# A hybrid decoder layer on one core: short matmul operands filled up with zero rows, and four stretches reordered

## The chip, the core and the metric

The kernel runs on one core of one Trainium2 chip. The metric is device microseconds of one execution of the whole program. The kernel before took 2721.23 us (median of 3 runs, 2720.73 to 2722.72). A core has five engines that run side by side, each with its own instruction queue: TensorE (PE; its weight loads are listed as PEld), VectorE (DVE), ScalarE (ACT), GpSimd (POOL) and SyncE (SP), which here only starts transfers.

## What is computed

One layer of a decoder trunk, for 1024 prompt tokens with 16 learned meta tokens ahead of them, and for a sample group of 8 sequences with 8 tokens each (1104 tokens in all, width 1024). Cut to its parts:

```
h = h + 0.5 * post1(swiglu1(pre1(h)))                  # d_ff 2816
u = pre_mix(h);  qkv, z, b, a, sq, sk, sv, g_dn, g_swa = split(u @ w_in)
A: gated DeltaNet, 8 heads of 128 (chunks for the prompt, a recurrence from a given
   state s0 for each of the 8 sample sequences), gated RMSNorm with silu(z)
B: sliding-window attention, window 128 plus the 16 meta keys, 8 query heads
y = sigmoid(g_dn) * o_A + sigmoid(g_swa) * o_B
h = h + post_mix(y @ w_out)
h = h + 0.5 * post2(swiglu2(pre2(h)))
```

Besides y the outputs are the convolution, DeltaNet and window states of both groups.

## The kernel before, in words

**Order of work.** TensorE's instructions run in the order in which the program is written; the other engines' order is chosen when the program is built, except where an instruction is pinned to program order. The written order comes from `weave`: each stream of work is a generator with a start share, an end share and a number of steps, and the steps of all streams are merged by these shares. A projection of 72 or 73 steps is typically the filler between the dependent steps of another stream. The products of activations by weights are done in three fast passes (high by high, high by low, low by high parts); the small products of the mixer are plain float32 and appear in the trace as two matmul records each.

**Stages, with the time from the span's start.** First FFN: gate and up to about 485 us, `Ffn.down` (L511) to about 765. The last feature group of `down` ends in 24 steps; then each of nine token tiles (eight of 128, one of 80 tokens) is turned to token rows by `end` (L588, transposes L579), normed and added (`post_norm`: ACT square L81, two POOL instructions, DVE L625 and L626), stored, normed again (`pre_norm`, DVE L100) and transposed back in two steps (PE L104, then ACT L119 and DVE L120). `tail_steps` takes a list: a number is `end` of that tile, a pair such as (0,) one step of its `pre_norm`, None nothing. The lists stand in `body` beside `weave`, and in the three lists handed to `Mixer.before` (L795), where the filler is the first projections.

**Keys.** `all_keys` (L1026) projects the eight heads' keys one after the other. The generator `gates` (L813) has four steps and computes decays from a small product: matmuls L820; a long run of small DVE instructions; matmuls L858 to L863 with DVE L866; then ACT L870, the transpose L872, a store and six ACT exponentials. The first runs beside the first weave, the other three beside the projection of key head 2.

**Window attention.** `swa_block` (L1194) runs 32 times, from about 1055 to 1315 us. Its last step (L1252) accumulates four to seven products in one bank; the first of them has 48 rows: the 16 meta keys' values `vm` in three parts, by the transposed probabilities `ptm`. `swa_sample` (L1258) runs twice, each time with two halves; a half has four pairs of matmuls (L1311 with 128 rows, L1312 with 24 rows), each pair on its own 32 columns of the array. The triangular solves of the DeltaNet (`lane_solve`, DVE L1061 and L1063) run beside the first half of this stage.

**Heads.** `heads` (L1634) runs eight heads from about 1337 to 1880 us. Per head: `chain` (L1515, 29 steps, each waiting for the one before through ACT and DVE), `prep` and `prep8` of the next head, `emit` of the head before, and two projections as filler (`qv_steps`, `z_gate`). The sample group's part has 64 token rows and 16 meta rows: L1502 makes p8, L1543 solves with 80 rows, L1549 starts the state S from the 16 meta rows, L1552 makes the outputs from 64 rows, L1600 updates the eight sequences' states twice per head, 4 sequences at a time, from 64 rows of kd by `xe` (POOL L1559: the solution repeated eight times under `smask`). `emit` transposes the outputs (L1617; the sample's from partitions 64 to 127).

**Merge.** `z_gate` of the last head also loads `w_out` piece by piece (`load_w` L1686) into the memory of activations that are no longer needed. `begin` and `begin_last` do tile 0, `run` the others in the order 4, 1, 5, 2, 8, 6, 3, 7: `load` (L1786) brings y of all eight heads with one transfer, ACT L1715 and DVE L1716 split it, `tile_` (L1798) multiplies the two halves of the output one after the other.

The lines that speak most of the order around the change:

```
dn = f1.down(GROUPS, [(accp, (1, 2, 5, 7, 3, 6, 4))], hbp)
weave((dn, 0, 1, 15), ends(0, None, 1, None, None, (0,), (0,), 2, None, (1,), (1,), 3))
m.before([[ends((2,), (2,), 4, (3,), (3,), 5)], [ends((4,), (4,), 6, (5,), (5,), 7, 8)],
          [ends((6,), (6,), (7,), (7,), (8,), (8,))]])
```

Of the kernel before, what the change touches and what calls it, by code (L numbers as in the profile page):

```python
# [13 lines left out]
ALU = mybir.AluOpType  # L14
# [60 lines left out]
def rstd(c, pool, x, n, scale, eps, tag, dump=None, pin=lambda op: op):  # L75
# [5 lines left out]
    c.last_square = pin(nc.scalar.activation(dump[:n], x[:n], AF.Square, accum_out=r[:n])).ins  # L81
    nc.gpsimd.tensor_scalar(out=r[:n], in0=r[:n], scalar1=scale, scalar2=eps, op0=ALU.mult, op1=ALU.add)
    c.last_factor = nc.gpsimd.tensor_tensor(out=r[:n], in0=r[:n], in1=c.mhalf[:n, 0:1], op=ALU.pow).ins
# [87 lines left out]
class Ffn:  # L171
# [325 lines left out]
    def down(self, groups, accp, hbp):  # L497
# [9 lines left out]
        for vi, group in enumerate(groups[:-1]):  # L507
# [10 lines left out]
            for p in runs:  # L518
# [22 lines left out]
             for name in ("11", "21", "12", "22")}  # L541
        adds = [[(pool, 6, 1), (dve, 2, 1)], [(dve, 3, 5), (pool, 7, 6)], [(dve, 3, 6)], [(pool, 4, 7)], [(dve, 5, 7)], [], [],
# [110 lines left out]
C_BASE = C_SMASK + 8  # L653
# [5 lines left out]
def constants():  # L659
# [14 lines left out]
    cst[:64, C_SMASK:C_SMASK + 8] = seq[:64, None] == np.arange(8)[None, :]  # L674
# [19 lines left out]
class Mixer:  # L694
    def __init__(self, c, xT, I, O, es, ba_w):
# [10 lines left out]
        self.smask = t([P, 8], "smask")  # L706
        nc.sync.dma_start(self.smask, I["cst"][:, C_SMASK:C_SMASK + 8])
# [91 lines left out]
    def before(self, rest):  # L799
# [6 lines left out]
        with tc.issue_after(self.c.last_square), tc.issue_after(self.c.last_factor):  # L806
            self.ready[9] = self.w_in(9, raw[1])
# [5 lines left out]
    def gates(self, tp):  # L813
# [31 lines left out]
        for m in (15, 13, 11, 9, 7, 5, 3):  # L845
# [8 lines left out]
                                in1=self.smask[:80].unsqueeze(2).to_broadcast([80, 8, H]), op=ALU.mult)  # L854
# [171 lines left out]
    def all_keys(self):  # L1026
        c = self.c
        with ExitStack() as ek:
# [3 lines left out]
            with ExitStack() as eg:  # L1032
# [5 lines left out]
                before = [(gates, 0.5, 1, 3)]  # L1038
# [61 lines left out]
    def swa_kv(self, pool, tmp):  # L1100
# [6 lines left out]
        self.vm = c.t(pool, [48, 256], F32R, tag="vm")  # L1107
# [53 lines left out]
        nc.vector.tensor_copy(self.vm, vm)  # L1161
# [30 lines left out]
    def swa_block(self, t, p, pool):  # L1192
# [37 lines left out]
        pm = c.t(pool, [48, 2, P], F32R, tag="ptm", bufs=2)  # L1230
        nc.scalar.copy(pm, pt[:48, 0:2])
# [34 lines left out]
    def swa_sample(self, g, pool, tmp):  # L1266
# [27 lines left out]
        for half in range(2):  # L1294
# [109 lines left out]
    def persistent(self, pool):  # L1404
        c, nc = self.c, self.nc
        self.ms = [c.t(pool, [P, 8, P], tag=f"ms{i}") for i in range(1)]
        self.p8 = [c.t(pool, [64, P], tag=f"p8{i}") for i in range(2)]
        for m in self.ms + self.p8:
            nc.gpsimd.memset(m, 0.0)
# [68 lines left out]
    def prep8(self, h, pool):  # L1478
# [8 lines left out]
        kd = x["kd8"] = T([P, P], "kd8")  # L1487
        nc.sync.dma_start(kd, self.kd_d[h][:, 8, :])
        s0 = x["s0"] = T([P, 8, P], "s0")
# [13 lines left out]
        nc.vector.scalar_tensor_tensor(out=p8[:, 64:P], in0=pk[:64, 0, 0:64], scalar=self.s[:64, h, 8:9], in1=dt8,  # L1503
# [3 lines left out]
        self.pack8(x8, x["cv"])  # L1507
        vs = x["vs8"] = T([P, P], "vs8")
# [5 lines left out]
    def chain(self, h, pool):  # L1514
# [4 lines left out]
        vs, kd, s0, ms, p8 = (x[k] for k in ("vs8", "kd8", "s0", "ms", "p8"))  # L1519
# [35 lines left out]
        on = T([P, 1, P], "on8")  # L1555
        normed(o, slice(64, P), 8, 0, on)
        x["on"].append((on, 8, 1, 64))
        xe = T([64, 8, P], "xe")
# [580 lines left out]
```

## Time and profile before

| | |
|---|---|
| median of 3 runs | 2721.23 us |
| the profiled execution, device time | 2728.27 us |
| its span in the trace | 2726.4 us |
| mean granted TensorE clock | 0.989 of full |
| PE, PEld busy | 2644.8 us (97%), 2483.8 us (91%) |
| DVE, POOL, ACT busy | 1554.8, 1309.5, 1112.8 us |

The profiled execution is 7.0 us longer than the median of the runs. In the trace a PE row's duration overlaps that of the next row, since matmuls are pipelined; what an instruction costs is read from the starts. A form such as 48\*128 48x256 means 48 rows and 128 stationary columns, 256 moving columns; x2 at the end of a row means two records.

### The profile page before, as it was taken

To read this page: it belongs to the slowest core of one execution; us is meant where nothing else is said; L and a number is where in the kernel's file an instruction comes from. 1 tells how busy PE (TensorE), PEld (TensorE's weight loads), DVE (VectorE), ACT (ScalarE), POOL (GpSimd) and SP (SyncE) were. 2 spreads that over 40 slices of the span, in tenths; PEclk is the share of its full clock that TensorE was granted. 3 is DMA by queue.
4 is the path that set the end of the run, shared out by engine and by line. 5 is a ranking of instruction groups with operands and counts; after the bars stand their busy time and mean duration, and the time that the engine had idled before them with its cause. 6 is when DMAs were issued, how large, how long until landed. Compare 5 with 4: busy or idle time off the path is not lost. (4 is left out here: it accounts for less than half of the span.)

```text
span 2726.4 us, 49217 instructions
## 1 busy us (share of the span) xinstructions
PE 2644.8 (97%) x18957; PEld 2483.8 (91%) x18957; DVE 1554.8 (57%) x2294; ACT 1112.8 (41%) x2647; POOL 1309.5 (48%) x1227
## 2 busy tenths in 40 slices
PE   7999999999989998999999999998999999999998
PEld 7999999999978997887788888886789999999998
DVE  7656566446566769934354444443556556563566
ACT  6334343422145634555444444444543333344221
POOL 6655555445426733423344443344456555554471
PEclk9999999999999999999999999999999999999999
DMA  4344343677544743443333333334443344338764
GB/s 168 105 155 158 121 157 114 254 232 243 176 132 144 237 137 112 144 150 111 87 90 97 98 95 93 97 96 136 136 137 140 121 153 159 131 122 310 240 235 141
DMA packets 229552, 406.46 MB, mean 149 GB/s; under 512 B 59734, under 2 KB 121334, under 8 KB 229030
## 3 DMA queue, kind: packets, MB, share of 16 engines
q1 hardware_dynamic: 209014, 324.75, 36.9%
q10 hardware_dynamic: 20304, 78.56, 7.3%
q8 instruction: 150, 2.46, 0.4%
q14 instruction: 84, 0.69, 0.1%
HBM read 264.36 MB, written 140.53 MB: 149 GB/s over the span
## 5 line engine op out<-in xcount | busy, mean ns | idle before, releaser
L132 PE MATMUL gu<-xh,wl 128*128 128x512 f32 (+3 forms) x1456 | 497.3, 342 | 0.2 <-POOL wl L764 0.2
L128 PE MATMUL gu<-xh,wh 128*128 128x512 f32 (+3 forms) x1456 | 493.8, 339 | 0.0
L130 PE MATMUL gu<-xl,wh 128*128 128x512 f32 (+3 forms) x1456 | 493.4, 339 | 0.0
L282 POOL TENSOR_TENSOR wl<-T,wh 128x512 fp32r<-128x512 f32 x246 | 330.9, 1351 | 323.8 <-ACT wh L281 242.5
L492 PE MATMUL y<-hb,wh 128*128 128x256 f32 (+2 forms) x2528 | 430.6, 290 | 6.9 <-DMA hb<-hid 4.7
L282 POOL TENSOR_TENSOR wl<-raw,wh 128x512 fp32r<-128x512 f32 x200 | 282.8, 1422 | 257.5 <-ACT wh L281 202.4
L492 PEld LDWEIGHTS y<-hb,wh 128*128 128x128 f32 x2528 | 365.8, 188 | 9.0 <-DMA hb<-hid 4.5
L132 PEld LDWEIGHTS gu<-xh,wl 128*128 128x128 f32 x1456 | 277.7, 191 | 28.9 <-issue 11.1
L281 ACT CAST wh<-T 128x512 fp32r<-128x512 f32 x246 | 152.4, 620 | 369.3 <-PE B L316 114.3
L130 PEld LDWEIGHTS gu<-xl,wh 128*128 128x128 f32 x1456 | 278.1, 191 | 18.9 <-issue 1.2
L128 PEld LDWEIGHTS gu<-xh,wh 128*128 128x128 f32 x1456 | 278.0, 191 | 18.4 <-issue 1.6
L492 PE MATMUL y<-hb,wl 128*128 128x256 f32 (+2 forms) x1264 | 271.5, 288 | 0.0
L281 ACT CAST wh<-raw 128x512 fp32r<-128x512 f32 x200 | 122.3, 620 | 276.3 <-PE C L316 86.7
L503 DVE TENSOR_TENSOR acc<-acc,y 128x552 f32<-128x552 f32 (+4 forms) x216 | 144.9, 679 | 145.2 <-PE y L492 144.8
L764 POOL TENSOR_TENSOR wl<-raw,wh 128x1024 fp32r<-128x1024 f32 x60 | 146.5, 2441 | 160.2 <-ACT wh L763 153.3
L492 PEld LDWEIGHTS y<-hb,wl 128*128 128x128 f32 x1264 | 207.0, 188 | 0.0
L256 DVE TENSOR_TENSOR T<-raw,raw 128x512 f32<-128x512 f32 x124 | 118.8, 962 | 114.7 <-POOL wl L282 114.7
L1530 POOL TENSOR_TENSOR f<-f,mhalf 128x1 f32<-128x1 f32 (+1 forms) x72 | 54.8, 761 | 112.6 <-DVE f L1528 107.3
L267 DVE TENSOR_TENSOR T<-raw,T 128x512 f32<-128x512 f32 x62 | 64.4, 1041 | 62.7 <-POOL wl L282 62.3
L922 DVE SCALAR_TENSOR_TENSOR cv<-pc,cw,cv 128x1131 f32<-128x1131 f32 x48 | 67.0, 1397 | 29.3 <-POOL cv L919 28.9
L256 DVE TENSOR_TENSOR T<-raw,T 128x512 f32<-128x512 f32 x62 | 64.3, 1044 | 33.6 <-POOL wl L282 33.4
L1061 DVE TENSOR_TENSOR ltmp<-la 72x14 f32<-72x14 f32 (+37 forms) x76 | 69.6, 916 | 12.7 <-DMA la<-b_d 11.3
(588 smaller groups left out, 7323.7 us busy)
## 6 DMA issues: line engine op xcount, KB each, us to landing
hb<-hid SPq DMA_DIRECT2D x71, 552.0 KB
hb<-hid SPq DMA_DIRECT2D x71, 544.0 KB
hid<-hs ACTq DMA_DIRECT2D x69, 552.0 KB
hid<-hs ACTq DMA_DIRECT2D x69, 544.0 KB
raw<-in_w_in_dram SPq DMA_DIRECT2D x58, 512.0 KB
raw<-in_ffn_w_gate_dram SPq DMA_DIRECT2D x100, 256.0 KB
raw<-in_ffn_w_up_dram SPq DMA_DIRECT2D x94, 256.0 KB
raw<-in_ffn_w_down_dram SPq DMA_DIRECT2D x88, 256.0 KB
```

The lines of the kernel that those rows point to most:

```text
L128: nc.tensor.matmul(ps, wh, xh, start=first and i == 0, stop=False)
L130: nc.tensor.matmul(ps, wh, xl, start=False, stop=False)
L132: nc.tensor.matmul(ps, wl, xh, start=False, stop=last and i == n - 1)
L256: pin(self.nc.vector.tensor_tensor(out=b[name], in0=b[x], in1=b[y], op=ALU.subtract))
L267: nc.vector.tensor_tensor(out=s, in0=b["21"], in1=s, op=ALU.subtract)
L281: self.nc.scalar.copy(hi, s)
L282: self.nc.gpsimd.tensor_tensor(out=lo, in0=s, in1=f32(hi), op=ALU.subtract)
L492: self.nc.tensor.matmul(self.view(ps[d], (i,)), w[x][:, d * P:(d + 1) * P], hb[:, y, lo:hi], start=j + x + y == 0, stop=j == len(items) - ...
L503: dve = lambda out, x, y: nc.vector.tensor_tensor(out=out, in0=x, in1=y, op=ALU.add)
L764: nc.gpsimd.tensor_tensor(out=lo, in0=raw, in1=f32(hi), op=ALU.subtract)
L922: nc.vector.scalar_tensor_tensor(out=cv, in0=pc[:, w:w + PADW], scalar=self.cw[:, j, w:w + 1], in1=cv, op0=ALU.mult, op1=ALU.add)
L1061: nc.vector.tensor_tensor(out=t, in0=a[:n, 0:j, j:j + 1].to_broadcast([n, j, w]), in1=a[:n, j:j + 1, j + 1:size].to_broadcast([n, j, w]), ...
```

## The change

It does six things. (1) Operands with 16, 24, 48 or 64 rows become operands of 80 or 128 rows whose added rows are zero, or lie where full-height operands are read: `vm` and `ptm` (now two buffers zeroed once), p8, the stationary side of L1502, the transposes of the sample outputs. The 24-row matmuls L1312 stay, but the four L1311 of a half are issued first and then the four L1312. (2) The mask that picked a sequence moves from the moving operand (`xe`, POOL, removed) to the keys: `kds`, nine masked copies of the 80 key rows made on ACT in `prep8`, pinned to program order; a product with 512 moving columns becomes four with 128. (3) In the first `down`, the hidden values of the last two products get four buffers of their own in the memory of the raw weights, one PSUM pool is given up two steps earlier, and the lists of tile steps change. (4) The second step of the four of `gates` is placed at 0.5 of the next projection, the last two at 0.99. (5) The last head's `z_gate` ends at 0.95 of the chain in place of 0.85. (6) The merge's tile 4 is loaded, split and multiplied in two parts: heads 0 to 6, then head 7, both output halves in each.

```diff
@@ Ffn.down
-    def down(self, groups, accp, hbp):
+    def down(self, groups, accp, hbp, last_hbp=lambda hbp: hbp):
...
+        hbp2 = last_hbp(hbp)
...
-        second = [self.values(hbp, group, p) for p in (8, 4)]
+        second = [self.values(hbp2, group, p) for p in (8, 4)]
...
-                for ds in ((0, 1), (2,), (3,)) if i == 0 and q == 4 else ((0,), (1,), (2,), (3,)):
+                for ds in ((0, 1), (2,), (3,)) if i == 0 and q == 4 and hbp2 is hbp else ((0,), (1,), (2,), (3,)):
@@ Mixer.before
-        with tc.issue_after(self.c.last_square), tc.issue_after(self.c.last_factor):
+        with tc.issue_after(self.c.squares[-2]), tc.issue_after(self.c.factors[-2]):
@@ all_keys
-                before = [(gates, 0.5, 1, 3)]
+                before = [(steps_of(gates, 1), 0.4, 0.6, 1), (gates, 0.98, 1, 1)]
@@ swa_kv, swa_block
-        self.vm = c.t(pool, [48, 256], F32R, tag="vm")
+        self.vm = c.t(pool, [P, 256], F32R, tag="vm")
+        self.pm = [c.t(pool, [P, 2, P], F32R, tag=f"ptm{i}") for i in range(2)]
+        for x in (self.vm, *self.pm):
+            nc.gpsimd.memset(f32(x), 0.0)
...
-        pm = c.t(pool, [48, 2, P], F32R, tag="ptm", bufs=2)
-        nc.scalar.copy(pm, pt[:48, 0:2])
+        pm = self.pm[t % 2]
+        nc.scalar.copy(pm[0:48], pt[:48, 0:2])
@@ swa_sample
                 nc.tensor.matmul(po[r], p[:, 0, r], vc[:, i, :], start=True, stop=False, tile_position=(0, 32 * i))
+            for i in range(4):
+                r = slice(32 * i, 32 * i + 32)
                 nc.tensor.matmul(po[r], p[:24, 1, r], v24[:, i, :], start=False, stop=True, tile_position=(0, 32 * i))
@@ prep8
+        kds = x["kds"] = T([80, 9, P], "kds")
+        def masked(ss):
+            for s in ss:
+                c.tc.keep_in_program_order(nc.scalar.activation(kds[:, s], kd[:80], AF.Copy,
+                                                                scale=self.smask[:80, s:s + 1]))
...
+        masked(range(4))
...
-        nc.tensor.matmul(pk[:64, 0, 0:64], kq[:, 0:64], kq[:, 64:P], start=True, stop=True)
+        nc.tensor.matmul(pk[:, 0, 0:64], kq, kq[:, 64:P], start=True, stop=True)
...
+        masked(range(4, 9))
@@ chain
-        nc.tensor.matmul(pu, kd[64:80], xs8[64:80], start=True, stop=True)
+        nc.tensor.matmul(pu, kds[:, 8], xs8[:80], start=True, stop=True)
...
-        nc.tensor.matmul(po, p8, xs8[0:64], start=True, stop=True)
+        nc.tensor.matmul(po, p8, xs8[:80], start=True, stop=True)
...
-        nc.gpsimd.tensor_tensor(out=xe, in0=xs8[0:64].unsqueeze(1).to_broadcast([64, 8, P]),
-                                in1=self.smask[:64].unsqueeze(2).to_broadcast([64, 8, P]), op=ALU.mult)
...
-                nc.tensor.matmul(pu, x["kd8"][0:64], xe[:, 4 * half:4 * half + 4, :], start=True, stop=True)
+                for s in range(4):
+                    nc.tensor.matmul(pu[:, s, :], kds[:, 4 * half + s], xs8[:80], start=True, stop=True)
@@ emit
-                r = slice(0, P) if w == P else slice(64, P)
-                nc.tensor.transpose(pt[:, i, :w], on[r, i, :], self.k(C_IDENT)[r, r])
+                nc.tensor.transpose(pt[:, i, :], on[:, i, :], self.k(C_IDENT))
@@ heads
-                streams += [(self.z_gate(H - 1, pool, mg.load_w), 0, 0.85, 145), (steps_of(out, 2), 0.6, 1.15, 2)]
+                streams += [(self.z_gate(H - 1, pool, mg.load_w), 0, 0.95, 145), (steps_of(out, 2), 0.6, 1.15, 2)]
@@ Merge.load, Merge.tile_
+        for ks in (slice(0, H - 1), slice(H - 1, H)) if t == 4 else (slice(0, H),):
+            nc.sync.dma_start(f32(yl)[:, ks, :n], y[ks, :, t % 4 * P:t % 4 * P + n].rearrange("h p t -> p h t"))
...
+        if t == 4:
+            both = [c.t(self.psum, [P, 512], tag="dn", bufs=2) for _ in range(2)]
+            for ks in (range(H - 1), range(H - 1, H)):
+                for half in range(2):
+                    yield from self.mm(both[half], yh, yl, half, n, ks, ks.start == 0, ks.stop == H)
+                    if ks.stop == H:
+                        self.nc.scalar.copy(o[:n, half * 512:(half + 1) * 512], both[half])
@@ body
-        drain(steps_of(dn, 10))
+        drain(steps_of(dn, 8))
...
-        weave((dn, 0, 1, 15), ends(0, None, 1, None, None, (0,), (0,), 2, None, (1,), (1,), 3))
+        weave((dn, 0, 1, 17), ends(0, 1, None, None, None, (0,), (0,), 2, (1,), (1,), 3, None, None, (2,), (2,), 4))
...
-        m.before([[ends((2,), (2,), 4, (3,), (3,), 5)], [ends((4,), (4,), 6, (5,), (5,), 7, 8)],
-                  [ends((6,), (6,), (7,), (7,), (8,), (8,))]])
+        m.before([[ends(5, (3,), (3,), 6, (4,), (4,))], [ends(7, (5,), (5,), 8, (6,), (6,))],
+                  [ends(None, (7,), (7,), None, (8,), (8,))]])
```

## Rows read from the trace of the kernel before

**Rows 1.** The page, part 1: busy time, share of the span, instructions.

```profile
PE 2644.8 (97%) x18957; PEld 2483.8 (91%) x18957; DVE 1554.8 (57%) x2294; ACT 1112.8 (41%) x2647; POOL 1309.5 (48%) x1227
```

**Rows 2.** PE's waits, 730 to 850 us: total us, times, longest.

```profile
PE tr L872 <- ACT gc L870: 4.5, 1, 4.5
...
PE y L492 <- DMA hb<-hid: 1.7, 2, 1.3
```

**Rows 3.** Stretches: length, busy PE, PEld, DVE, ACT, POOL (instructions), granted clock, DMA, GB/s.

```profile
765.00:815.00 50.00, 39.29 (x304) 36.96 (x304) 31.36 (x35) 25.30 (x50) 17.10 (x33) 0.93 0.46 148
...
835.00:850.00 15.00, 10.52 (x53) 9.79 (x53) 9.72 (x11) 5.87 (x17) 4.81 (x8) 0.77 0.41 111
1000.00:1140.00 140.00, 131.50 (x808) 117.60 (x807) 136.41 (x189) 55.86 (x160) 53.18 (x48) 0.98 0.34 106
...
1340.00:1860.00 520.00, 517.68 (x3412) 453.37 (x3412) 231.18 (x489) 232.12 (x758) 211.21 (x254) 1.00 0.32 93
1860.00:1880.00 20.00, 14.72 (x81) 12.42 (x82) 9.46 (x22) 9.64 (x28) 16.00 (x16) 0.83 0.32 100
1888.00:1896.00 8.00, 5.23 (x16) 3.61 (x15) 2.65 (x3) 4.22 (x6) 1.87 (x3) 0.79 0.92 314
```

**Rows 4.** Timeline of PE, a window block: start us, us, line, operands, records.

```profile
1092.48 0.39 PE L132 MATMUL gu<-xh,wl 128*128 128x512 f32 x1
1092.80 0.38 PE L1252 MATMUL po<-ptm,vm 48*128 48x256 f32 x1
...
1093.92 0.40 PE L128 MATMUL gu<-xh,wh 128*128 128x512 f32 x1
```

**Rows 5.** Timeline of PE, one half of the sample attention.

```profile
1207.81 0.41 PE L1311 MATMUL po<-kc,pts 128*32 128x128 f32 x2
...
1210.48 0.41 PE L128 MATMUL gu<-xh,wh 128*128 128x320 f32 x1
1210.73 0.31 PE L130 MATMUL gu<-xl,wh 128*128 128x320 f32 x1
```

**Rows 6.** Timeline of PE, the sample scores: four column tiles, issued together.

```profile
1182.10 0.47 PE L1287 MATMUL sc<-kc,qp 128*32 128x152 f32 x8
1182.49 0.50 PE L128 MATMUL gu<-xh,wh 128*128 128x512 f32 x1
```

**Rows 7.** Timeline of PE, a state update with 64 rows.

```profile
1358.77 0.40 PE L128 MATMUL gu<-xh,wh 128*128 128x512 f32 x1
1359.00 0.40 PE L130 MATMUL gu<-xl,wh 128*128 128x512 f32 x1
1359.33 1.12 PE L1600 MATMUL on<-xe,kd 64*128 64x512 f32 x2
...
1360.72 0.40 PE L128 MATMUL gu<-xh,wh 128*128 128x512 f32 x1
```

**Rows 8.** Timeline of PE, the products with 16 and 64 rows.

```profile
1343.15 0.39 PE L130 MATMUL gu<-xl,wh 128*128 128x512 f32 x1
1343.47 0.48 PE L1549 MATMUL ch<-xs,kd 16*128 16x128 f32 x2
...
1344.63 0.28 PE L128 MATMUL gu<-xh,wh 128*128 128x256 f32 x1
```

**Rows 9.** Timeline of PE, the solve with 80 rows.

```profile
1340.83 0.39 PE L130 MATMUL gu<-xl,wh 128*128 128x512 f32 x1
1341.06 0.38 PE L1543 MATMUL ch<-vs,r 80*80 80x128 f32 x2
...
1341.51 0.40 PE L128 MATMUL gu<-xh,wh 128*128 128x512 f32 x1
```

**Rows 10.** ACT's scaled copy of one line: duration ns min, median, max; first and last start.

```profile
L1531 ACT ACTIVATE on<-o,f x72: 389/402/427, 1347.0 to 1877.7; 128x128 f32<-128x128 f32 x64, 64x128 f32<-64x128 f32 x8
```

**Rows 11.** PE's waits, 1858 to 1900 us: total us, times, longest.

```profile
PE ch L1584 <- ACT xs L1581: 3.4, 4, 2.0
```

**Rows 12.** Timeline of ACT, 1858 to 1900 us: start us, us, line, operands, instructions.

```profile
1868.80 1.65 ACT L1698 CAST xh<-raw 128x512 fp32r<-128x512 f32 x3
```

More of the change, by code (lines that the diff above doesn't have):

```diff
@@ L80, in rstd @@
         dump = c.t(pool, [P, D], BF16, tag="dump", bufs=1)
-    c.last_square = pin(nc.scalar.activation(dump[:n], x[:n], AF.Square, accum_out=r[:n])).ins
+    c.squares.append(pin(nc.scalar.activation(dump[:n], x[:n], AF.Square, accum_out=r[:n])).ins)
     nc.gpsimd.tensor_scalar(out=r[:n], in0=r[:n], scalar1=scale, scalar2=eps, op0=ALU.mult, op1=ALU.add)
-    c.last_factor = nc.gpsimd.tensor_tensor(out=r[:n], in0=r[:n], in1=c.mhalf[:n, 0:1], op=ALU.pow).ins
+    c.factors.append(nc.gpsimd.tensor_tensor(out=r[:n], in0=r[:n], in1=c.mhalf[:n, 0:1], op=ALU.pow).ins)
     return r
@@ L652 @@
 C_SMASK = 7 * P
-C_BASE = C_SMASK + 8
+C_BASE = C_SMASK + 16
 C_BASE0 = C_BASE + 272
@@ L705, in __init__ @@
         t = lambda shape, tag, dt=F32: c.t(kp, shape, dt, tag=tag)
-        self.smask = t([P, 8], "smask")
-        nc.sync.dma_start(self.smask, I["cst"][:, C_SMASK:C_SMASK + 8])
+        self.smask = t([P, 9], "smask")
+        nc.sync.dma_start(self.smask, I["cst"][:, C_SMASK:C_SMASK + 9])
         self.cw = t([P, 24, 4], "cw")
@@ L1406, in persistent @@
         self.ms = [c.t(pool, [P, 8, P], tag=f"ms{i}") for i in range(1)]
-        self.p8 = [c.t(pool, [64, P], tag=f"p8{i}") for i in range(2)]
-        for m in self.ms + self.p8:
+        self.p8 = [c.t(pool, [80, P], tag=f"p8{i}") for i in range(2)]
+        self.on8 = c.t(pool, [P, 1, P], tag="on8")
+        for m in (*self.ms, *self.p8, self.on8):
             nc.gpsimd.memset(m, 0.0)
@@ L1518, in chain @@
         x = self.hd[h]
-        vs, kd, s0, ms, p8 = (x[k] for k in ("vs8", "kd8", "s0", "ms", "p8"))
+        vs, kds, s0, ms, p8 = (x[k] for k in ("vs8", "kds", "s0", "ms", "p8"))
         so = T([P, 9], "so", 2)
@@ L1615, in emit @@
             for i in range(n):
-                r = slice(0, P) if w == P else slice(64, P)
-                nc.tensor.transpose(pt[:, i, :w], on[r, i, :], self.k(C_IDENT)[r, r])
+                nc.tensor.transpose(pt[:, i, :], on[:, i, :], self.k(C_IDENT))
             zc = Z[:, t0 * P:t0 * P + n * w].rearrange("p (i w) -> p i w", w=w)
-            nc.vector.scalar_tensor_tensor(out=zc, in0=pt[:, :n, :w], scalar=self.nw, in1=zc, op0=ALU.mult,
+            nc.vector.scalar_tensor_tensor(out=zc, in0=pt[:, :n, P - w:], scalar=self.nw, in1=zc, op0=ALU.mult,
                                            op1=ALU.mult)
@@ L1790, in load @@
         y = self.m.y_d[t - t % 4]
-        nc.sync.dma_start(f32(yl)[:, :, :n], y[:, :, t % 4 * P:t % 4 * P + n].rearrange("h p t -> p h t"))
         yh = c.t(pool, [P, H, P], F32R, tag="yh")
-        if n == 64:
-            self.pair(yh, yl)
-        else:
-            self.split(yh, yl, slice(0, H), n)
+        for ks in (slice(0, H - 1), slice(H - 1, H)) if t == 4 else (slice(0, H),):
+            nc.sync.dma_start(f32(yl)[:, ks, :n], y[ks, :, t % 4 * P:t % 4 * P + n].rearrange("h p t -> p h t"))
+            if n == 64:
+                self.pair(yh, yl)
+            else:
+                self.split(yh, yl, ks, n)
         return yh, yl, n
@@ L1800, in tile_ @@
         c, pool = self.c, self.pool
-        for half in range(2):
+        if t == 4:
[5 more added lines that the diff above has]
+                        self.nc.scalar.copy(o[:n, half * 512:(half + 1) * 512], both[half])
+        for half in range(2) if t != 4 else ():
             ps = c.t(self.psum, [P, 512], tag="dn", bufs=2)
@@ L1945, in body, with last_hbp @@
         f1.tp = c.pool(eb, "T", bufs=6, side="right")
-        f1.rawp = c.pool(eb, "raw", bufs=10, side="right")
         hbp = c.pool(eb, "hb", bufs=5, side="right")
+        er = ExitStack()
+        f1.rawp = c.pool(er, "raw", bufs=10, side="right")
+        def last_hbp(_):
+            er.close()
+            return c.pool(eb, "hb2", bufs=4, side="right")
         f1.psy = [c.pool(eb, "psy0", bufs=2, space=PSUM), c.pool(ep, "psy1", bufs=2, space=PSUM, side="right")]
@@ L1958, in finish1 @@
             yield from pre_norm(c, pool, psum, y, f1.left_over(t, res), n, gain("mix_norm_pre", pool),
-                                to_chunk(c, uT[WHERE[t][0]], t))
-        dn = f1.down(GROUPS, [(accp, (1, 2, 5, 7, 3, 6, 4))], hbp)
+                                lambda ps: to_chunk(c, uT[WHERE[t][0]], t)(ps))
+        dn = f1.down(GROUPS, [(accp, (1, 2, 5, 7, 3, 6, 4))], hbp, last_hbp)
         drain(steps_of(dn, 28 * 2))
```

17 lines of the change are left out of this document (8 added, 9 removed).

## The prediction

> **What bounds the kernel now.** I read the busy shares first. PE is busy for 97% of the span, DVE for 57%, POOL 48%, ACT 41% [rows 1]: the end is set by PE's own queue, and time can go only where PE works longer than it must, waits, or runs at the lower clock. So I read three things next: PE's waits, the stretches in which PE is not busy or the granted clock is under 1.00, and the starts of PE's small matmuls among the projections.
>
> The starts are the surprise. A projection step with 512 columns follows the one before after 0.23 us [rows 7] (so 0.12 for 256 columns, 0.15 for 320). From the last projection step before the 48-row product of a window block to the first after the block, 1.44 us pass for that step, the 48-row product and six products with 256 columns [rows 4]. Less 0.23 and 6 x 0.12, the 48-row product has cost 0.49 us; one with 128 rows costs 0.12. The records call all of it busy. The 80-row solve shows that it is not the shortness as such: from the step before it to the second step after it 0.68 us pass; less two steps, its two records cost 0.22, or 0.11 each [rows 9]. So 80 rows run like 128, and 16, 24, 48 and 64 rows pay something on the way in and out.
>
> The waits and the clock stand in five stretches [rows 3]. At the end of the first FFN (765 to 815 us) PE idles 50 - 39.3 = 10.7 us and the clock is 0.93, which is 0.07 x 50 = 3.5 us. Around the gates (835 to 850) it idles 4.5 us, nearly all of it one wait for the copy gc [rows 2], and the clock takes 0.23 x 15 = 3.4. At the end of the last chain (1860 to 1880) it idles 5.3 and the clock takes 3.4. At the merge's second tile (1888 to 1896) it is 2.8 and 0.21 x 8 = 1.7. From 1000 to 1140 us DVE is busy 136.4 of 140 us. Through the heads, 1340 to 1860, PE idles only 2.3 us of 520.
>
> **The change part by part, as PE time taken away.**
>
> *Window blocks.* 32 blocks, each 0.49 - 0.12 = 0.37: 11.8 us. The zeroing is three POOL instructions, once.
>
> *Sample attention.* From the first L1311 of a half to the second projection step after it 2.92 us pass; less 0.15 for one step it is 2.77 [rows 5]. Four column tiles of 128 rows issued one behind the other show what a group costs: eight records and the way to the next step in 0.39 us [rows 6]. Two groups and the late second step after them (some 0.1) make 0.88, so 1.89 saved, by four halves: 7.6 us. If the 24-row group does not run side by side, a half saves about 1.0; that is the lower bound, 4 us.
>
> *State updates.* An update with 64 rows takes 1.72 us between the projection steps, less two steps 1.26 [rows 7]. The four products that replace it are eight records of 0.11 [rows 9], 0.88. Saved 0.38, 16 times: 6.1 us.
>
> *The 16-row and 64-row products* of the chain take 1.48 us, less two steps 1.02 [rows 8]; four full-height records cost 0.44. Saved 0.58, 8 times: 4.6 us. L1502 and the sample's transposes in L1617 are one entry and exit per head each; no row is kept for them, the nearest is [rows 8], where two products lose 0.58. I take 0.3 a head for both together (bounds 0 and 0.58): 2.4 us.
>
> That makes 32.5 us. It will not all arrive: nine of the 32 blocks lie before 1140 us, where DVE is full with the solves [rows 3] and does not get faster; what PE saves there it will wait for DVE. I take off 9 x 0.37 = 3.3: **29 us** (24 to 33).
>
> The rows have two kinds of cost in them, and a page explains one against this change. An update's two 64-row records start about 0.5 us apart, where 512 columns of float32 should stream in less, so the weight load seems to stand in the open there [rows 7], and in the 80-row solve it does not [rows 9]. The Trainium skill (TensorE: Matmul & The Clock Gate, part 3, The mechanism) says that a weight load runs beside matmuls in flight only if it goes to other row groups; by that, full-height records would expose every load too and the four small products, with four times the loads, would be a loss. Rows 9 speak against it; it returns below as a rival.
>
> *The masks on ACT.* Per head nine instructions; the nearest, a scaled copy of 64 to 128 rows by 128, takes 0.40 us [rows 10]. 72 x 0.40 = 29 us of ACT, which in the heads' stretch is busy 232 of 520 us [rows 3]; xe leaves POOL. They are pinned, in bursts of 4 and 5 (1.6 and 2.0 us), so what is queued behind them is the chain's copy xs, for which PE waits. Their own input kd is no longer read by PE, its buffer is free as soon as the masks are made, and its load can go out almost a head earlier; I expect no wait for it. Cover: the five or so projection steps between two chain steps, about 1.2 us with 512 columns. I take 0.2 us for each of 14 bursts beside a chain (bounds 0 and 1.0): **-2.5 us** (0 to -14).
>
> *End of the first FFN.* Each tile's `end` brings a load, eight transposes, two ACT, four POOL and three DVE instructions and a store; three of these steps (tile 2's two and 4's `end`) move from the projections into `down`. Nothing is removed from PE; what changes is the lead: 4 or 5 list items from `end` to the first transposes before, 7 items now for all but tile 4 (5). The waits of 10.7 us plus 3.5 of clock should mostly go, and the hidden values' own buffers remove 1.7 us of waiting for their load [rows 2]: 15.9 at most. DVE limits it: it was busy 31.4 of these 50 us, and is busy for 80% if PE needs only 39. Also the first `end` now comes two steps earlier behind the last adds, perhaps 1 us. I take **11 us** (3 to 16).
>
> *Gates.* The transpose moves from 0.75 to 0.99 of a projection, whose 24 x 3 steps take 24 x (0.23 + 0.12 + 0.15) = 12 us: 2.9 us of the 4.5 us wait are covered so, more if DVE's order improves with the earlier second step. The store of gc, the six exponentials and the next head's decays, which queue behind it on SP, ACT and POOL, come later relative to PE; the slack of the products that use them is unknown to me, some 0 to 2 us late. Of 7.9 I take **5.5** (2 to 8).
>
> *Last chain.* With the filler to 0.95 instead of 0.85, about 1.5 chain steps stand bare instead of 4.4. The waits for xs there are 3.4 us [rows 11]; one of 2.0 stands behind three ACT casts of the output weights, 1.65 us [rows 12], which will now come at the very end. Two transfers, four ACT and four POOL instructions move 6 us later and are needed only in `begin`, about 8 us on. Of 8.7 us I take **3** (0 to 8).
>
> *Merge.* Heads 0 to 6 of tile 4 (a transfer, an ACT and a DVE instruction) no longer wait for the last head's store; 42 matmuls of 0.23 cover head 7. But both banks now end together and the next tile waits for their copies. Of 4.5 I take **3.5** (1 to 4.5).
>
> Sum: 29 - 2.5 + 11 + 5.5 + 3 + 3.5 = 49.5 us. The profiled execution took 2728.3 us, so it would take 2678.8; it is 7.0 above the median, so the median should come to 2671.8, **2672 us**. About 0.2% (5.4 us) is what a measurement of this kernel can tell from no change.
>
> **The rivals.**
> *Only the short operands count.* The stretches keep their waits because DVE's queue, not the position of PE's steps, sets them; DVE at 80% and the shared loads speak for it, the longer leads against. 49.5 less 23, and 26.5 stays: 2695 us.
> *The small products show their weight loads.* Then a full-height record costs 0.21, as 0.11 of load are added to 0.11: updates lose 16 x (8 x 0.21 - 1.26) = 6.7 instead of winning 6.1, the chain's products win 1.4 instead of 4.6: 16 us less, 2688 us. Rows 9 speak against it. It is what the page's rule would do here.
> *Row height is not the cause* but something else in those products, such as float32 operands among the fast ones: then padding removes nothing from 24 us, and four products for one add work: 2701 us. The solve in rows 9 is float32 too and pays nothing.
> *Slower: the bursts stop the chain.* Place: the chain's xs behind 4 or 5 pinned masks. One ACT run of 1.65 us ahead of xs did cost 2.0 us of waiting [rows 11, 12], and the clock in that stretch fell to 0.83, another 3.4. At 5.4 us a burst, 14 bursts cost 76 us, and the time is 2671.8 + 2.5 + 76 = 2750 us. It decides from (49.5 + 2.5) / 14 = 3.7 us a burst. Against it: that run stood where no filler was left, and elsewhere PE hardly waits [rows 3].
> *All waits and clock losses go*: 33 + 16 + 8 + 8 + 4.5 = 69.5, 2652 us.
>
> **How the numbers follow.** Forecast 0.64, only short operands 0.20, open weight loads 0.04, other cause 0.03, slower 0.03, all waits gone 0.06. The range from 2656 to 2696 leaves out the last three and the ends of the forecast's own (2657 to 2688). Faster by over 0.2%: 0.96; within: 0.01; slower: 0.03.
>
> **What would show it.** L1252's first product and the next one 0.12 us apart; the eight L1311 records within 0.2 us of one another; four products of 128 columns in 0.9 us where L1600 stood; gc's wait gone from the list and the clock near 1.00 from 835 to 850; no wait at 1888 to 1896. The prediction is wrong if PE waits on xs through the heads, if new DVE waits stand between 740 and 815 us, or if full-height records lie 0.2 us apart.

## The result, and the profile after

The changed kernel took 2689.89 us (median of 4 runs, 2687.11 to 2691.37) against 2721.97 us for the kernel before: 32.1 us less, ratio 0.9877, 95% interval 0.986 to 0.9894. A second time, beside other runs, it took 2689.60 against 2722.36. The forecast was 2672 us, the range 2656 to 2696. So the sign and the range held, and of 49.5 us expected 32.1 came.

The page of the kernel after, part 1, answers to [rows 1]:

```profile
span 2685.2 us, 49482 instructions
...
PE 2604.9 (97%) x19053; PEld 2483.4 (92%) x19053; DVE 1556.6 (58%) x2295; ACT 1127.4 (42%) x2720; POOL 1290.1 (48%) x1223
```

The first reading is a subtraction. Span less PE's busy time was 2726.4 - 2644.8 = 81.6 us; it is 2685.2 - 2604.9 = 80.3 (78.0 in a second execution). PE is idle nearly as long as it was; what went is busy time. That is a first sign that the short operands paid. Of the moved steps the sum says little: the kernels below with the old order of steps are idle for 76.9 to 85.9 us, and one stretch can hide another. From 730 to 870 us, around the first FFN's end and the gates, PE's idle time did fall, from 140 - 122.4 = 17.6 to 140 - 128.8 = 11.2 us. The row of the kernel before, then that of the kernel after, in the columns of [rows 3]:

```profile
730.00:870.00 140.00, 122.39 (x863) 114.54 (x862) 85.62 (x114) 62.62 (x159) 52.96 (x83) 0.95 0.42 137
730.00:870.00 140.00, 128.75 (x911) 121.26 (x910) 98.95 (x132) 68.03 (x180) 60.20 (x90) 0.95 0.43 141
```

Elsewhere it grew.

The timeline of PE in the kernel after: a window block, a half of the sample attention and a state update, as [rows 4, 5, 7].

```profile
1079.29 0.40 PE L132 MATMUL gu<-xh,wl 128*128 128x512 f32 x1
1079.53 0.28 PE L1257 MATMUL po<-ptm,vm 128*128 128x256 f32 x1
1079.64 0.28 PE L1257 MATMUL po<-ptoh,vth 128*128 128x256 f32 x1
...
1080.35 0.40 PE L128 MATMUL gu<-xh,wh 128*128 128x512 f32 x1
...
1191.83 0.43 PE L1316 MATMUL po<-kc,pts 128*32 128x128 f32 x8
1192.18 0.42 PE L1319 MATMUL po<-v,pts 24*32 24x128 f32 x8
...
1192.79 0.31 PE L130 MATMUL gu<-xl,wh 128*128 128x320 f32 x1
...
1327.87 0.39 PE L130 MATMUL gu<-xl,wh 128*128 128x512 f32 x1
1328.10 1.05 PE L1615 MATMUL on<-xs,kds 80*128 80x128 f32 x8
...
1329.23 0.39 PE L128 MATMUL gu<-xh,wh 128*128 128x512 f32 x1
```

The block takes 1.06 us from step to step, not 1.44; the first product is 0.11 us ahead of the second. The half takes 0.96 - 0.15 = 0.81 us, not 2.77, and the 24-row group does run side by side. The update takes 1.36 - 0.47 = 0.89, not 1.26. All three are within 0.1 us of the prediction's 0.37, 1.89 and 0.38 saved.

PE's waits in the kernel after (total us, times, longest), from 730 to 870, 1100 to 1300 and 1800 to 1860 us:

```profile
PE tr L580 <- DVE y L626: 5.7, 1, 5.7
PE tr L976 <- DVE b L1012: 2.6, 1, 2.6
PE tr L104 <- DVE xl L120: 2.0, 1, 2.0
...
PE tr L873 <- ACT gc L871: 0.3, 1, 0.3
...
PE pt L1245 <- ACT ptm L1236: 2.7, 4, 0.8
...
PE ch L1598 <- ACT xs L1595: 5.5, 2, 2.9
PE dn L128 <- ACT yh L1729: 1.8, 1, 1.8
```

The wait for gc went from 4.5 to 0.3 us and the two for hb are gone [rows 2]. The longest ones now are 5.7 us for y and 2.6 for b, and in the last chain 5.5 for xs instead of 3.4 [rows 11]. The stretches that answer to [rows 3], in the same columns:

```profile
765.00:815.00 50.00, 42.22 (x312) 40.24 (x311) 29.60 (x40) 21.89 (x47) 13.01 (x27) 0.90 0.35 117
835.00:850.00 15.00, 15.00 (x101) 13.81 (x100) 10.23 (x11) 10.42 (x39) 13.34 (x12) 1.00 0.62 218
...
850.00:860.00 10.00, 7.38 (x38) 6.12 (x37) 5.52 (x11) 8.84 (x35) 7.18 (x12) 0.83 0.65 184
1000.00:1140.00 140.00, 130.45 (x829) 119.00 (x828) 137.05 (x204) 60.87 (x175) 50.34 (x54) 0.98 0.36 109
...
1815.00:1842.00 27.00, 19.51 (x115) 17.45 (x115) 10.48 (x25) 13.47 (x37) 18.48 (x18) 0.87 0.35 108
```

Around the gates PE is now full at clock 1.00, and the hole stands ten microseconds further on, with the clock at 0.83 (a mix of the two levels, 1.2 and 2.4 GHz). POOL was busy 4.8 of the 15 us there; it is busy 13.3 now. The rows compare the same times and not quite the same work: the first projection step with 512 columns starts at 818.2 us, before at 826.8.

To find which edit moved which stretch, I took six marks from the trace of every kernel: A, FFN1's first down product with 296 columns; B, the first projection step with 512 columns; C, the first with 320; D, the first window score; E, the heads' first product (L1436, tr<-rt,bo); F and G, the first product of the chain (L1569) of heads 1 and 7; H, the merge's first product; I, the last product of its high-by-high pass (L128). Line numbers are those of the kernel before. Lengths in us, worked out from the starts of these instructions (one execution each):

| | A to B | B to C | D to E | F to G | G to H | H to I |
|---|---|---|---|---|---|---|
| before | 314.0 | 105.5 | 291.9 | 423.9 | 59.7 | 97.5 |
| e3_window | 313.6 | 104.0 | 282.2 | 423.7 | 58.7 | 98.3 |
| e4_masks | 316.1 | 102.9 | 288.8 | 415.3 | 59.0 | 98.1 |
| e1_rows | 314.5 | 104.3 | 274.7 | 415.3 | 59.5 | 98.1 |
| e2_order | 305.9 | 105.7 | 288.7 | 423.4 | 59.1 | 96.9 |
| after | 306.6 | 103.7 | 273.5 | 415.0 | 61.0 | 96.3 |
| e11_again | 306.2 | 103.8 | 273.1 | 414.9 | 60.6 | 96.2 |
| e5_no_gates | 305.7 | 102.9 | 274.7 | 415.6 | 60.7 | 98.6 |
| e12_no_gates2 | 305.1 | 104.3 | 274.9 | 415.4 | 61.0 | 98.7 |
| e6_no_last | 304.2 | 105.3 | 273.4 | 415.4 | 59.8 | 97.8 |

How far one execution differs from another must be kept in mind. The kernel after and e11_again are the same kernel: they agree within 0.4 us in these columns, but from E to F, which the table leaves out, they take 83.0 and 87.0 us. In e7_casts and e8_decays below, A to B is 303.8 us, though neither has an edit there.

### The profile page after: what moved, and what is told of

The parts are those of the page before. It is cut to its first block, busy times and chain, and to the rows that moved or that the text cites. A ratio compares the mean times of both kernels' runs of the same rounds, so it can differ in the third digit from the quotient of the medians.

```text
span 2685.2 us, 49482 instructions
## 1 busy us (share of the span) xinstructions
PE 2604.9 (97%) x19053; PEld 2483.4 (92%) x19053; DVE 1556.6 (58%) x2295; ACT 1127.4 (42%) x2720; POOL 1290.1 (48%) x1223
## 5 line engine op out<-in xcount | busy, mean ns | idle before, releaser
L128 PE MATMUL gu<-xh,wh 128*128 128x512 f32 (+3 forms) x1456 | 492.9, 339 | 0.0
L128 PEld LDWEIGHTS gu<-xh,wh 128*128 128x128 f32 x1456 | 278.0, 191 | 16.6 <-issue 0.9
L1064 DVE TENSOR_TENSOR la<-la,ltmp 72x14 f32<-72x14 f32 (+37 forms) x76 | 75.3, 991 | 1.4
```

The source lines that it names most:

```text
L128: nc.tensor.matmul(ps, wh, xh, start=first and i == 0, stop=False)
L1064: nc.vector.tensor_tensor(out=a[:n, 0:j, j + 1:size], in0=a[:n, 0:j, j + 1:size], in1=t, op=ALU.add)
```

## The experiments

**Taking the change apart.** Four kernels built on the one before, each with some of the edits.

e1_rows: all the short operands, none of the moved steps.

```diff
+        self.vm = c.t(pool, [P, 256], F32R, tag="vm")
+        self.pm = [c.t(pool, [P, 2, P], F32R, tag=f"ptm{i}") for i in range(2)]
...
+            for i in range(4):
+                r = slice(32 * i, 32 * i + 32)
...
+        kds = x["kds"] = T([80, 9, P], "kds")
```

> The kernel before with the short operands filled up (window products, sample attention's two groups, the masked keys on ScalarE in place of xe) and none of the moved steps. Theory A, the prediction's own terms: 29 less 2.5 us, so about 2695.5 us, and the moved steps bring the rest. Theory B, the waits were only moved and the short operands are nearly the whole gain: 33 us, so 2687 to 2691 us, the same as the changed kernel within 3 us. Either way PE's waits at the first FFN's end, at gc and in the last chain should stand in its trace as in the kernel before.

Measured 2702.13 us (2696.86 to 2704.35) against 2721.30: 19.2 less, ratio 0.9925 (0.9913 to 0.9937). Neither theory: less than the 26.5 of A, much less than the 33 of B. In the table its stretches D to E and F to G are as short as in the kernel after; so part of what the products gave was lost elsewhere. The granted clocks say where: each run has its mean clock on record, and the mean of its six runs is 0.9873, against 0.9893 in the 17 of the kernel before. Over some 2700 us this is about 5 us more lost to the lower level (an estimate from these figures, as if TensorE set the pace throughout). At an equal clock the gain would be some 24 us, near A's 26.5.

e2_order: all the moved steps, none of the short operands.

```diff
+        second = [self.values(hbp2, group, p) for p in (8, 4)]
...
+                before = [(steps_of(gates, 1), 0.4, 0.6, 1), (gates, 0.98, 1, 1)]
...
+        streams += [(self.z_gate(H - 1, pool, mg.load_w), 0, 0.95, 145), ...]
...
+        for ks in (slice(0, H - 1), slice(H - 1, H)) if t == 4 else (slice(0, H),):
```

> The kernel before with all the moved steps (FFN1's end, gates, last z_gate, the merge's tile 4) and the short operands left as they were. Theory A: 11 + 5.5 + 3 + 3.5 = 23 us less, about 2699 us. Theory B: within 4 us of the kernel before, 2718 to 2726 us, with the wait for gc gone and others in its place (on DVE's products of the next keys, on xs behind the output weights' casts).

Measured 2712.46 us (2708.83 to 2715.86): 8.8 less, ratio 0.9964 (0.9952 to 0.9976). A's 23 is refuted, and so is B's "nothing". The table tells which part it is: A to B is 305.9 where four kernels with the old end have 313.6 to 316.1, some 9 less; B to C, G to H and H to I lie within their range or at most 0.6 outside it. Which edit of FFN1's end did it (the hidden values' own buffers, the lists, the PSUM pool given up earlier) was not tested. The mean clock of its runs is 0.9915, against 0.9893: by the estimate above some 6 of the 8.8 us are clock, so shorter holes and a higher clock came together.

e3_window: vm and ptm alone.

```diff
-        self.vm = c.t(pool, [48, 256], F32R, tag="vm")
+        self.vm = c.t(pool, [P, 256], F32R, tag="vm")
...
-        nc.scalar.copy(pm, pt[:48, 0:2])
+        nc.scalar.copy(pm[0:48], pt[:48, 0:2])
```

> The kernel before with vm and ptm filled up to 128 rows alone. 32 blocks by 0.37 us are 11.8 us; if DVE swallows what is saved in the nine blocks before 1140 us, 8.5 us: 2713.5 us. If nothing is swallowed 2710 us. If row height is not the cause, 2722 us.

Measured 2718.54 us (12 runs, 2713.94 to 2722.08): 2.8 less, ratio 0.9987 (0.9979 to 0.9996). Row height is the cause in the trace, but little arrives. Part of where it goes can be read in PE's waits from 1100 to 1290 us. First the kernel before and e2_order, whose blocks have 48 rows, then e3_window:

```profile
PE pt L1240 <- ACT ptm L1231: 1.8, 2, 1.1
PE pt L1241 <- ACT ptm L1232: 0.5, 2, 0.2
```

```profile
PE pt L1244 <- ACT ptm L1235: 2.9, 3, 1.3
PE pt L1244 <- DVE ptol L1247: 0.7, 1, 0.7
```

PE comes to the next tile's transposes 0.37 us earlier by each block, and ScalarE's copy of the meta keys' weights, which empties the buffer, seems not to come earlier; with 1.1 to 2.4 us this is a part of what is missing. D to E shrinks by 9.7 us against the kernel before and by 6.5 and 6.6 against e2_order and e4_masks, not by 11.8. The median gained less still, 2.8 us, but at a lower clock: the mean of the twelve runs is 0.9875, against 0.9893, again some 5 us by the estimate above. At an equal clock the gain would be near 8 us, about the 8.5 expected. Why the clock is lower is not shown. The profiled execution, 2713.94 us, was the fastest of the twelve.

e4_masks: the masked keys, the four small products and the filled p8, kq and on8.

```diff
-                nc.tensor.matmul(pu, x["kd8"][0:64], xe[:, 4 * half:4 * half + 4, :], start=True, stop=True)
+                for s in range(4):
+                    nc.tensor.matmul(pu[:, s, :], kds[:, 4 * half + s], xs8[:80], start=True, stop=True)
```

> The kernel before with the masked keys on ScalarE, the four small products, and the filled p8, kq and on8 alone; the window products and the sample attention stay. Prediction's terms: 6.1 + 4.6 + 2.4 less 2.5 for the masks, 10.6 us: 2711 us. If the masks on ScalarE cost PE nothing: 13.1 us, 2709 us. If the bursts of masks stop the chain by more than 0.9 us each: no gain or a loss, 2722 us or more. If full-height records show their weight loads: 2724 us or more.

Measured 2711.35 us (2707.69 to 2713.93): 10.0 less, ratio 0.996 (0.9948 to 0.9972). The predicted 10.6 holds. F to G is six heads: (423.9 - 415.3) / 6 = 1.43 us each, 11.5 for eight. Without any cost of the masks 13.1 were expected, so by these stretches they cost PE some 1.6 us. In one place they do what was feared: in the kernel after, seven of them stand ahead of xs in head 0's chain, and PE waits 0.8 us.

```profile
1353.83 1.27 ACT L1502 ACTIVATE kds<-kd,smask 80x128 f32<-80x128 f32 x4
...
1355.26 0.98 ACT L1502 ACTIVATE kds<-kd,smask 80x128 f32<-80x128 f32 x3
1356.14 0.25 ACT L1595 COPY xs<-ch 128x128 f32<-128x128 f32 x1
```

**Putting single moves back in the kernel after.** e5_no_gates and, once more, e12_no_gates2, beside the unaltered kernel e11_again:

```diff
-                before = [(steps_of(gates, 1), 0.4, 0.6, 1), (gates, 0.98, 1, 1)]
+                before = [(gates, 0.5, 1, 3)]
```

> The changed kernel with the gates' steps put back (all three spread from 0.5 to 1 of the first projection). Theory A, the prediction's term: 5.5 us slower, 2695.4 us. Theory B, the wait for gc (4.5 us) was exchanged for waits behind the decays that now come later: within 2.5 us of the changed kernel, 2687.5 to 2692.5 us, with the wait for gc back in the trace and the wait of 2.6 us for b gone from it.

> The changed kernel once more, unaltered, beside the next run. Its median should be 2687 to 2692 us; the same waits (5.7 us at 774, 2.6 at 855, 2.9 and 2.7 on xs) should stand in its trace, and whatever differs from the first trace by more than 1 us in a stretch is what one execution differs from another.

> The changed kernel with the gates' steps put back, once more, beside the unaltered one. In the first run it was 4.4 us slower, but its stretch from the first FFN's end to the first pieces of the next heads was not longer in the trace. If the gates' move brings 4 to 5 us, it is again 4 to 5 us slower than the run beside it. If it brings nothing (the wait for gc exchanged for the one for b), the two lie within 2 us.

Measured 2694.27 (2690.31 to 2694.99) and 2692.91 us (2689.47 to 2697.79), e11_again 2689.60 (2686.60 to 2697.24): without the move 4.4 and 3.3 us slower, with ranges that overlap. Yet the gates' own stretch is not longer without it: A to C is 408.6 and 409.4 us, with it 410.3 and 410.0. The wait for gc is back (3.0 and 4.5 us) and the one for b is gone, as theory B had it. The time that is missing without the move lies a thousand microseconds later, in code that is the same: in H to I (98.6 and 98.7 against 96.3 and 96.2) and in the heads' start, where the clock differs. Windows of e12_no_gates2 and of the kernel after, from E to the first product of head 0's chain, the columns as in [rows 3]:

```profile
1295.00:1319.30 24.30, 20.89 (x124) 17.60 (x124) 3.39 (x12) 10.39 (x36) 4.80 (x6) 0.86 0.40 105
```

```profile
1293.60:1314.90 21.30, 18.14 (x124) 14.93 (x123) 3.42 (x12) 10.38 (x36) 4.89 (x6) 1.00 0.44 120
```

The same 124 instructions take 24.3 us at a clock of 0.86 and 21.3 at 1.00. In e11_again, the same kernel as after, it is 0.92. These are single executions: the two without the move were the slowest of their runs, that of the kernel after was the fastest. Over all runs the mean clock is 0.9875 and 0.9878 without the move, 0.9900 and 0.9894 with it, by the estimate above 7 and 4 us, as much as the whole difference. So what the move seems to bring is clock elsewhere and not the wait that it was made for. Whether the move sets this clock, or chance, stays open.

e6_no_last: the last z_gate and the merge's tile 4 as before.

```diff
-        streams += [(self.z_gate(H - 1, pool, mg.load_w), 0, 0.95, 145), ...]
+        streams += [(self.z_gate(H - 1, pool, mg.load_w), 0, 0.85, 145), ...]
...
-        for ks in (slice(0, H - 1), slice(H - 1, H)) if t == 4 else (slice(0, H),):
```

> The changed kernel with the last z_gate back at 0.85 and the merge's tile 4 back in one load and one split. Theory A: 3 + 3.5 us slower, 2696.4 us. Theory B, xs waits behind the output weights' casts either way and the early load of tile 4 stands behind the last head's stores in SP's queue: within 2.5 us, 2687.5 to 2692.5 us; xs then waits in several pieces of 0.5 to 2.2 us in place of two of 2.7 to 2.9.

Measured 2688.74 us (2684.82 to 2690.57), 1.2 less than the kernel after: these two moves bring nothing that the runs show. Theory B holds; xs now waits four times, 4.2 us in all, the longest 1.8.

**Why the waits stayed: the last chain.** The timeline of ACT in the kernel after:

```profile
1817.57 3.21 ACT L1712 CAST xh<-raw 128x512 fp32r<-128x512 f32 x6
1820.67 0.26 ACT L1595 COPY xs<-ch 128x128 f32<-128x128 f32 x1
...
1832.86 2.16 ACT L1712 CAST xh<-raw 128x512 fp32r<-128x512 f32 x4
1834.93 0.26 ACT L1595 COPY xs<-ch 128x128 f32<-128x128 f32 x1
```

Six and four casts of the output weights, in the order that the build chose, stand ahead of xs; the two waits of 2.9 and 2.7 us are theirs. e7_casts deals them out by hand:

```diff
+                    for n, _ in enumerate(self.proj_piece(w, WHOLE[i], evac(first), 1088)):
+                        if self.casts and n % 5 == 4:
+                            self.casts.pop(0)()
+                        yield
...
-                nc.scalar.copy(wh[:, cols], raw[:, cols])
+                c.tc.keep_in_program_order(nc.scalar.copy(wh[:, cols], raw[:, cols]))
```

> The changed kernel with the 16 casts of the output weights kept in program order on ScalarE and dealt out one to every five projection steps, the last four beside begin's products. If the runs of six and of four casts ahead of xs are what stops the last chain, the waits of 2.86 and 2.69 us go, and with them most of the 3.3 us of low clock there: 5 to 8 us faster, 2682 to 2685 us. If the chain's own latency sets that stretch once the fillers run out, the waits are spread over more places and the time stays at 2688 to 2692 us.

Measured 2680.84 us (2676.50 to 2686.30): 9.1 less than the kernel after. G to H falls from 61.0 to 53.3 us. Here too the clock rose with the waits gone: 0.9925 in the mean of its runs, 0.9900 in those of the kernel after, some 7 us by the estimate above. PE's waits there, 1790 to 1850 us:

```profile
PE dn L128 <- ACT yh L1744: 1.8, 1, 1.8
PE on L1635 <- ACT on L1553: 1.7, 1, 1.7
...
PE ch L1602 <- ACT xs L1599: 0.9, 2, 0.5
```

The wait for yh, 1.8 us, is left: the merge's. SP's issues in the kernel after show why the split load did not remove it:

```profile
1839.78 0.32 SPq L1639 DMA_DIRECT2D y_d<-Z  x1
...
1844.32 0.32 SPq L1639 DMA_DIRECT2D y_d<-Z  x1
1844.73 3.56 SPq L1807 DMA_DIRECT2D yl<-y_d  x2
```

The load of heads 0 to 6 is issued right behind the last head's second store, 0.41 us after it, since both stand on SP's queue; it needs nothing of that store. An earlier load was not tried.

**Why the waits stayed: the gates and FFN1's end.** The timelines of DVE and of POOL in the kernel after, at both holes:

```profile
766.08 3.41 DVE L627 SCALAR_TENSOR_TENSOR y<-y,rp,res 128x1024 f32<-128x1024 f32 x1 [0.81 <-POOL rp L83]
...
844.88 3.45 DVE L992 TENSOR_TENSOR kt<-kt,sd 128x1152 f32<-128x1152 f32 x1
848.25 3.84 DVE L927 SCALAR_TENSOR_TENSOR cv<-th,cv 128x1131 f32<-128x1131 f32 x1
...
766.01 2.39 POOL L765 TENSOR_TENSOR wl<-raw,wh 128x1024 fp32r<-128x1024 f32 x1
...
844.68 2.43 POOL L951 TENSOR_TENSOR dt<-dt,cst 128x1024 f32<-128x1024 f32 x1
...
848.50 2.39 POOL L951 TENSOR_TENSOR dt<-dt,cst 128x1024 f32<-128x1024 f32 x1
```

At 766.08 DVE starts 0.07 us after POOL and takes 3.41 us, nearly POOL's 2.39 and its own 1.28 one after the other. The Trainium skill (SBUF — State Buffer, Who interferes with whom) says that a DVE instruction with two inputs in SBUF and a GpSimd instruction that reads SBUF contend for one shared pair of ports, and that whichever starts first has it for its whole length. The row agrees. The later pair is less plain: DVE's L927 starts at 848.25 while a small addition on POOL (L953, 1.47 us from 847.07) still runs, and POOL's next large one follows at 848.50; DVE's ends at 852.09, behind both. Two kernels take one of the two partners away or move it.

e8_decays:

```diff
+        eng = nc.vector if h < 2 else nc.gpsimd
-        pin(nc.gpsimd.tensor_tensor(out=dt[:, 0:8, :], in0=dt[:, 0:8, :],
+        pin(eng.tensor_tensor(out=dt[:, 0:8, :], in0=dt[:, 0:8, :],
```

> The changed kernel with the decays' two additions of heads 0 and 1 on VectorE in place of GpSimd. If VectorE's products for the keys are late because two of its instructions stretch from 1.35 to 3.4 and 3.8 us while GpSimd adds the masks (2.4 us each), those come back to their 1.35 us, PE's wait of 2.6 us for b at 854 us goes, and with the clock behind it some 4 us: 2685 to 2688 us. If VectorE is late by the sheer number of its instructions there, the two additions (1.2 us each or more) make it later still: 2690 to 2693 us and a longer wait for b.

Measured 2684.53 us (2682.83 to 2686.99): 5.4 less than the kernel after. PE's waits from 735 to 860 us:

```profile
PE tr L580 <- DVE y L626: 5.7, 1, 5.7
...
PE tr L873 <- ACT gc L871: 1.9, 1, 1.9
```

The wait for b is gone although DVE does more: its two instructions fall from 3.45 to 1.35 us and from 3.84 to 2.51. The wait for gc is back by 1.9; in e6_no_last, which has no edit here, the two waits are 1.9 for gc and 1.0 for b. B to C, where the edit lies, is 101.8 us, 1.9 less and the least of all kernels here, and 101.8 again in e10_best. That much is the repair's; where the rest of the 5.4 us comes from is not shown (A to B, ahead of the edit, is 2.8 shorter, as in e7_casts).

e9_late9:

```diff
-        with tc.issue_after(self.c.squares[-2]), tc.issue_after(self.c.factors[-2]):
+        with tc.issue_after(self.c.squares[-1]), tc.issue_after(self.c.factors[-1]):
```

> The changed kernel with the second projection weight's split held back behind the last square and factor of the norms issued so far, not the last but one. PE's longest wait, 5.7 us at 774 us, ends with VectorE's product y, queued behind an instruction that took 3.41 us while GpSimd's split of that weight (2.39 us) ran, and takes 1.28 us elsewhere. If the two engines hold each other up, that instruction comes back to 1.28 us, the wait falls to about 3.6 us: some 2 us faster, with the clock up to 3.7, 2686 to 2688 us. If the instruction is late for another reason (its input res, the factor), nothing changes: 2690 us, the wait at 5.7 us.

Measured 2688.73 us (2687.21 to 2691.89), 0.9 less than e11_again, which is less than these runs can tell. The mechanism is plain in the timelines of DVE and POOL all the same:

```profile
766.11 1.28 DVE L627 SCALAR_TENSOR_TENSOR y<-y,rp,res 128x1024 f32<-128x1024 f32 x1 [0.81 <-POOL rp L83]
...
769.65 3.44 POOL L765 TENSOR_TENSOR wl<-raw,wh 128x1024 fp32r<-128x1024 f32 x1
```

DVE's instruction is back at 1.28 us, and now POOL's takes 3.44: this time DVE had started first (L100, at 769.59). PE's wait for y falls from 5.7 to 4.1 us, so 1.6 of it were POOL's doing; another, for b of the next head, grows from 0.6 to 2.2.

**The three repairs together**, e10_best (e7, e8 and e9 in one):

> The changed kernel with three repairs together: the output weights' casts dealt out in the last chain (alone 9.1 us faster), the decays' additions of heads 0 and 1 on VectorE (alone 5.4), the second weight's split held back (some 2). If they add, 2673 us; if the clock's recoveries were counted twice, 2676 to 2680 us.

Measured 2676.32 us (2675.52 to 2679.24) against 2722.36: ratio 0.9833 (0.9813 to 0.9854), 13.3 less than e11_again beside it. The three singles add to 15.4. Span less busy time is 2677.3 - 2605.5 = 71.8 us, the least of all kernels here. It beats both the kernel before and the one after.

## Why the prediction was right and wrong

**Right: that the short operands are slow by their height, and the price of each.** The three readings from the starts came within 0.1 us. By stretches, D to E lost 291.9 - 273.5 = 18.4 us, or 15.3 against the 288.8 and 288.7 of two kernels with the same blocks; the steps for windows and sample attention, 11.8 + 7.6 - 3.3, made 16.1. The sample attention alone, e1_rows against e3_window, is 282.2 - 274.7 = 7.5 us. The heads lost 1.43 us each, 11.5, where 10.6 was written. The rival of the open weight loads is refuted: an 80-row record of the update costs 0.89 / 8 = 0.11 us, where by the rule of the Trainium skill (TensorE: Matmul & The Clock Gate, part 3, The mechanism) it would have been 0.21, as the prediction read it; the measurement decides. The same section of the Trainium skill also lets a load go ahead into a background weight buffer, which the prediction left out and which fits the 0.11. The slower rival, bursts of masks at 3.7 us or more, is refuted by the one wait of 0.8.

Height is not the whole of it. L1502 has 128 rows and, in the kernel before, 64 stationary columns:

```profile
1808.32 0.39 PE L130 MATMUL gu<-xl,wh 128*128 128x512 f32 x1
1808.64 0.33 PE L1502 MATMUL tr<-kq 128*64 128x64 f32 x2
...
1809.24 0.39 PE L128 MATMUL gu<-xh,wh 128*128 128x512 f32 x1
```

Less two steps, its two records cost 0.46 us; with 128 columns, in the kernel after, they cost 0.22 (0.68 us from step to step). So a narrow stationary side paid here too. Prediction and change filled it up, but the account by rows alone does not cover it.

**About right in the windows' size, wrong in the place: the swallower.** The step said that nine blocks before 1140 us would lose their gain to DVE, 3.3 us. PE's idle time from 1000 to 1140 rose only from 8.5 to 9.6 us; waits stand after 1140 us too, on ScalarE's copy of ptm: 2.9 us in e3_window from 1100 us, against 0.5 (e2_order), 1.1 (e4_masks) and 1.8 (before). By D to E the term gave 6.5 to 9.7 us for 8.5; alone, the median gave 2.8 (interval of the ratio 0.9979 to 0.9996), some 8 by the estimate at an equal clock.

**Wrong: the moved steps, 8.8 us for 23.** Term by term, from the table:
*FFN1's end*, 11 predicted: A to B is 314.6 in the mean of the four kernels with the old end and 305.6 in the six with the new, 9.0. A good size, 2 of it inside the down products, where the waits for hb went; but the longer leads did not end the waits: from 765 to 815 us 7.8 us are idle for 10.7, 5.7 of them one wait for y, whose product is queued on DVE behind another tile's; POOL's hold-up made 1.6 of the 5.7.
*Gates*, 5.5 predicted: B to C did not shrink (104.0 in the mean of the six kernels with the old step, 104.6 in the four with the new); without the move the whole is 3.3 and 4.4 us slower, at places that it does not touch and by a lower clock. The prediction named the decays on POOL as what comes later and gave them "some 0 to 2 us". The wait for b, 2.6 us with the clock at 0.83 around it, stands there now, as they fell beside two large DVE instructions. The failed step is that slack; two engines that hold each other up were not in the sum.
*Last chain*, 3 predicted: G to H is 60.6 to 61.0 us in the four kernels below e2_order in the table that have the two late moves, 59.1 in e2_order, which has them too, and 58.7 to 59.8 without them. The step that failed is "will now come at the very end", of three casts: there are sixteen, and the build put ten of them ahead of xs in two runs. With the casts dealt out the stretch gives 7.7 us, so the cover was there.
*Merge*, 3.5 predicted: 1.8 + 0.4 us of waiting are left of 2.8. The step "no longer wait for the last head's store" forgot SP's queue, on which the load stands behind that store.

**The sum.** 19.2 and 8.8 make 28.0; the whole gave 32.1. The 4 us between are about what these medians can be off. The time fell between the forecast, 18 us away, and the rival that only short operands count (2695 us), 5 us away; the range held because it was wide enough for that rival, and the sum behind the forecast was not right. The rival's reason, DVE's queue, fits the gates and what is left of the waits at FFN1's end; there it missed the 9 us that did come, and in the last chain and the merge it was ScalarE's order and SP's queue.

## What to carry to other kernels

A step moved to cover a wait moves all that it issues: list its partner engines' instructions at the new place, and ask which of them run beside a large instruction of the neighbour that shares their ports, and what stands ahead of its transfer on the queue. Where the build orders an engine, look in the trace for runs of equal instructions ahead of the one copy that a chain waits for, and deal them out by hand. And read span less busy time early, but by stretches: here the sum moved by 1.3 us, while 6.4 had gone from 730 to 870 us and come back elsewhere.

## What was not expected of the hardware

Two engines lengthened each other's instructions, by nearly the other's whole duration: DVE's from 1.28 to 3.41 us beside POOL's 2.39, and, with the order reversed, POOL's from 2.39 to 3.44. And the granted clock of a stretch far from any edit differed from one execution to the next (0.86 in e12_no_gates2, 0.92 and 1.00 in two executions of one kernel, for the same instructions in the heads' start), which moved it by up to 3 us; some of what single edits seem to bring or cost here is that.
